# Reordering splits and additions around two seven-product blocks of a transformer layer

## The chip, the cores and the metric

The kernel runs on one core of a Trainium2 chip. The metric is the device time of one execution in microseconds (us); before the change the median of three runs is 786.5 us. TensorE (PE) multiplies matrices into PSUM; VectorE (DVE), ScalarE (ACT) and GpSimd (POOL) do elementwise work; SyncE (SP) issues most of the transfers.

## The reference

One layer on 512 tokens of width 1024, all in float32. The input is normed and multiplied by one wide matrix, and the result is cut into the parts of two branches: a gated linear attention with four heads (gla) and a latent attention with eight heads (mla). The branches are gated, summed and projected, and a squared-ReLU network follows. The change touches the first part:

```python
n = rmsnorm(h, g_mix[l])
proj = n @ w_in[l]
(gq, gk, gv, gr, z_gf, z_gb, cq, ckv, kr, z_ma, z_mb) = jnp.split(proj, SPLIT_IDX, axis=-1)
# gla: per head, forward and backward in the tokens
la_f = jax.nn.log_sigmoid((z_gf @ w_gate_f + b_gate_f).astype(jnp.float32)) / GLA_GATE_NORM
b = jnp.cumsum(log_a, axis=3)
q_dec = q * jnp.exp(b)
k_dec = k * jnp.exp(-b)
```

## The kernel before

**Split products.** A float32 operand is written as high + low, both in the format that TensorE takes (fp32r). `split` (L92) makes the high part on ACT (L93) and the low part, source minus high, on DVE (L94). A product of two split operands is three matmuls: `mm3`, L88 to L90. So each weight needs an ACT and a DVE instruction before TensorE can use it. A split weight lies in the buffers `wh` and `wl`, four of each, shared by all products of this stretch; a weight as loaded lies in `wf`, three of them. A buffer is given to the next tile when its last reader is done.

**Seven products for eight.** The products for gr (gates of gla) and gv (its values), 512 tokens by 1024 columns each, are done with seven block products in place of eight (class `Seven`). `SEVEN` gives their order: 1, 2, 5, 6, 3, 7, 4; so "the sixth product" is number 7. A weight has four blocks, and each block two halves, so `prepare(m)` makes up to two subtractions of blocks on DVE (`less`, L601) and then two splits (tiles such as gr70h and gr71l: block gr, product 7, half 0 or 1, high or low). `product(m)` runs 24 matmuls of 512 columns onto two accumulators and then takes the sums: products 1, 5, 6 are copied out by ACT (L643); behind 2, 3, 7 DVE adds the accumulator to a copy (L650), and behind 2, 3, 7, 4 the finished rows go to a `sink`. For gr that is a tanh on ACT (L659) and a multiplication on DVE (L660); for gv a scaled split (L97, L98). Products 1, 6, 7, 4 share the accumulators `xs`; product 4 must wait until DVE has read them behind product 7.

**Fillers.** Between the block products stand small projections, called fillers: zb4, the z chunk (wz, result zk; the inputs of the gates and the rotary key), gq1, gk1, zb5. Each has a load, a split of 128x1024 (wz: 128x512) and 24 matmuls (zk: 16).

**The order.** The loop over `steps` runs gr's seven products and gv's first three. In each step the operands two steps ahead are prepared, then the product of this step is run; in a step with a filler, first the filler's load and split are written, then the product, then the preparation, then the filler's matmuls. The sums of the input (xy, xz) are split in steps 1 and 2. The last four products of gv are written out by hand and mixed with the decays of head 0: `gates_begin` (two matmuls, Abs, Exp, Ln on ACT), `gates_end` (for both directions four scans L453 and a subtraction L457 on DVE, two exponentials L461 and L462 and a small one on ACT, small copies on POOL), and `gla_qk`, which multiplies q and k by the decays (L482 on DVE, L490 on POOL). The first matmuls of the scores are bd (L521).

What sets the order: `in_program_order` (called with ACT and DVE as `SPLITTERS` from `fixed` on, with TensorE from `ordered` on) makes each of these engines run its instructions in the order in which they are written, up to the end of the loop over the heads. POOL is held in order up to the gates. SP is ordered by the planner; the fillers' loads are only held behind the loads of gr's blocks.

Of the kernel before, what the change touches and what calls it, by code (L numbers as in the profile page):

```python
# [56 lines left out]
def tile_block(ctx: ExitStack, tc: tile.TileContext, t, out: bass.AP):  # L57
# [13 lines left out]
    def u4(name, dt=F32R, shape=(P, 2, S)):  # L71
        return tl(list(shape), dt, "u4", 26, name)
# [4 lines left out]
    def ps(tag, name):  # L77
        serial[0] += 1
        return pp.tile([P, S], F32, tag=tag, bufs=4, name=f"{name}_{serial[0]}")
# [343 lines left out]
            nc.sync.dma_start(kr[a + 32 : a + 48, :], kr[a : a + HALF, :])  # L423


    def gates_begin(h):

        l = u4("l", F32)
        ms = []
        for i, d in enumerate(("f", "b")):  # L430
            bcol = (V_BF if d == "f" else V_BB) + h
            bias = gvec[:, bcol : bcol + 1]
            acc = ps("mm", f"gate{d}")
            nc.tensor.matmul(acc, gates[d][:, h * P : (h + 1) * P], z4, start=True, stop=True)
            nc.scalar.activation(l[:, i], acc, AF.Abs, bias=bias)
            m = u2(f"m{d}")
            nc.vector.tensor_scalar(m, acc, bias, 0.0, op0=ALU.add, op1=ALU.min)
            ms.append(m)
        nc.scalar.activation(l, l, AF.Exp, scale=-1.0)
        nc.scalar.activation(l, l, AF.Ln, bias=1.0)  # L440
        return l, ms

    def gates_end(begun):
        l, ms = begun
        return {d: decays(d, l[:, i], ms[i]) for i, d in enumerate(("f", "b"))}

    def decays(d, l, m):
        sign = 1.0 if d == "f" else -1.0
        rr = tl([P, NT, P + 1], F32, "rr", 2, f"rr{d}")
        nc.gpsimd.memset(rr[:, :, 0:1], 0.0)  # L450
        for j in range(NT):
            c = slice(j * P, (j + 1) * P)
            nc.vector.tensor_tensor_scan(rr[:, j, 1:], m[:, c], l[:, c], 0.0, ALU.add, ALU.subtract)  # L453
        dif = u2(f"dif{d}", F32, (P, NT, P))
        off = 1 if d == "f" else 0
        mid = rr[:, :, 64:65]
        nc.vector.tensor_tensor(  # L457
            dif, rr[:, :, off : off + P], mid.to_broadcast([P, NT, P]), op=ALU.subtract
        )
        ee = u4(f"ee{d}", F32, (P, 2, NT, P))  # L460
        nc.scalar.activation(ee[:, 0], dif, AF.Exp, scale=sign * INV_NORM)  # L461
        nc.scalar.activation(ee[:, 1], dif, AF.Exp, scale=-sign * INV_NORM)  # L462
        v3 = tl([P, 3, NT], F32, "v3", 4, f"v3{d}")
        nc.gpsimd.tensor_copy(v3[:, 0, :], rr[:, :, 64])  # L464
        nc.gpsimd.tensor_tensor(v3[:, 1, :], rr[:, :, P], rr[:, :, 64], op=ALU.subtract)
        nc.gpsimd.tensor_copy(v3[:, 2, :], rr[:, :, P])
        e3 = tl([P, 3, NT], F32, "e3", 4, f"e3{d}")
        nc.scalar.activation(e3, v3, AF.Exp, scale=INV_NORM)
        return ee, e3

    def project_qk(h, x):
        col, name = ((C_GQ, "gq"), (C_GK, "gk"))[x]
        qk[h, x] = qk_normed(h, x, proj_T(col + h * P, f"{name}{h}"))

    def gla_qk(h, parts):
        near = {}
# [107 lines left out]
    class Seven:  # L584
# [17 lines left out]
                    self.blocks[dst][g], self.blocks[x][g], self.blocks[y][g], op=ALU.subtract  # L602
                )

        def prepare(self, m):

            x = {1: 0, 2: 2, 5: 0, 6: 0, 3: 3, 7: 1, 4: 2}[m]
            if m == 5:
                self.less(0, 1, 0)
            elif m == 6:  # L610
                self.less(0, 3, 0)
            elif m == 3:
                self.less(2, 2, 0)
            elif m == 7:
                self.less(1, 3, 1)
            self.right[m] = []
            for g in range(2):
                wh, wl = halves(2, S, f"{self.name}{m}{g}")
                split(wh, wl, self.blocks[x][g])
                self.right[m].append((wh, wl))  # L620

        def product(self, m):
            if m == 1:
                self.xs = [ps("at", f"{self.name}x{rb}") for rb in range(2)]
                self.c11, self.c12, self.c22 = ([u2(f"{self.name}{c}") for _ in range(2)] for c in "abc")
            elif m == 2:
                self.ws = [ps("mm", f"{self.name}w{rb}") for rb in range(2)]
            elif m == 5:
                self.zs = [ps("at", f"{self.name}z{rb}") for rb in range(2)]
            accs = {2: "ws", 5: "zs", 3: "zs"}.get(m, "xs")  # L630
            accs = getattr(self, accs)
            begin = m in (1, 2, 5)
            right = self.right.pop(m)
            for p in range(KD // 2):
                lh, ll = x_left[p][m]
                wh, wl = right[p // 2]
                for rb in range(2):
                    tok = slice(rb * P, (rb + 1) * P)
                    mm3(accs[rb], lh[:, tok], ll[:, tok], wh[:, p % 2, :], wl[:, p % 2, :],
                        begin and p == 0, p == KD // 2 - 1, not begin)  # L640
            if m in (1, 5, 6):
                for acc, c in zip(accs, {1: self.c11, 5: self.c22, 6: self.c12}[m]):
                    nc.scalar.activation(c, acc, AF.Copy)  # L643
            elif m == 4:
                for rb, acc in enumerate(accs):
                    self.sink(2 + rb, 0, acc, u2(f"{self.name}d"))
            else:
                cs = {2: self.c11, 3: self.c12, 7: self.c22}[m]
                for acc, c in zip(accs, cs):
                    nc.vector.tensor_tensor(c, acc, c, op=ALU.add)  # L650
                for rb, c in enumerate(cs):
                    self.sink(rb + (2 if m == 7 else 0), int(m != 2), c, c)

    g1, v = {}, {}
# [298 lines left out]
    def finish_zb(f, begun):  # L953
        g2.append(gated(proj_run(begun, xT), f"b{f}")[1])
# [10 lines left out]
    finish_zb(2, zb_early[0])  # L965
    sevens[0].prepare(2)
    finish_zb(3, zb_early[1])
    for n, (a, m) in enumerate(steps[:-4]):
        ahead = steps[n + 2]
        if a == 0:  # L970
            for x in {3: (0,), 7: (2, 1), 4: (3,)}.get(m, ()):
                sevens[1].load(x)
        if (a, m) in fillers:
            first_part, rest = fillers[a, m]
            at = traced()
            w = first_part()
            goes_behind((at, traced()), loading, (mybir.EngineType.SP,))
            if n == 1:
                split_sums(x_y, 5, 6)
            sevens[a].product(m)  # L980
            sevens[ahead[0]].prepare(ahead[1])
            rest(w)
            continue
        if n == 2:
            split_sums(x_z, 7, 3)
        sevens[ahead[0]].prepare(ahead[1])
        if (a, m) == (0, 5):
            load_gates()
            pos_i = u2("pos_i", I32)
            nc.gpsimd.dma_start(pos_i, t["positions"][0].partition_broadcast(P))  # L990
        if (a, m) == (0, 4):
            split_gates()
        sevens[a].product(m)
    in_program_order(summed, (mybir.EngineType.Pool,))

    gated_now = gates_begin(0)
    sevens[1].prepare(7)
    sevens[1].product(6)  # L1000
    parts = gates_end(gated_now)
    sevens[1].prepare(4)
    sevens[1].product(3)
    w_k = begin_qk(1, 1)
    sevens[1].product(7)
    w_b = begin(C_ZB + 5 * P, "zb5")
    near, nxt, far = gla_qk(0, parts)
    finish_qk(1, 1, w_k)
    sevens[1].product(4)
    w_a = begin_za(0)  # L1010
    finish_zb(5, w_b)
    ckv_, cq_ = Latent(C_CKV, 2, V_KV, "ckv"), Latent(C_CQ, 3, V_Q, "cq")
    for h in range(GH - 1):
        sc = gla_scores(near, nxt, far)
        gated_now = gates_begin(h + 1)
        w_b = begin_za(2 * h + 1)
        acc = proj_run(w_a, xT)
        if h < 2:
            w_a, lows = begin_late(C_GQ + (h + 2) * P, f"gq{h + 2}")
        else:  # L1020
            ckv_.begun[0], lows = begin_late(C_CKV, "ckv0")
        l, ms = gated_now
        parts = {"f": decays("f", l[:, 0], ms[0])}
        lows()
        parts["b"] = decays("b", l[:, 1], ms[1])
        za_gate(2 * h, acc)
        os = gla_out(h, sc)
        near, nxt, far = gla_qk(h + 1, parts)
        rs = gla_squares(h, os)
        za_gate(2 * h + 1, proj_run(w_b, xT))  # L1030
        if h < 2:
            w_b = begin_qk(h + 2, 1)
            gla_gated(h, os, rs)
            finish_qk(h + 2, 0, w_a)
            w_a = begin_za(2 * h + 2)
            finish_qk(h + 2, 1, w_b)
        else:
            ckv_.begin(1)
            gla_gated(h, os, rs)
            ckv_.run(0)  # L1040
            cq_.begin(0)
            ckv_.run(1)
        gla_turn(h)
# [413 lines left out]
```

## Time and profile before

| | us |
|---|---|
| median of 3 runs (lowest, highest) | 786.5 (786.31, 787.09) |
| the profiled execution: its own time | 789.31 |
| its span, first to last instruction | 787.6 |
| PE busy | 766.8 (97%) |
| DVE busy | 569.7 (72%) |
| ACT busy | 442.1 (56%) |
| POOL busy | 113.2 (14%) |
| mean granted clock of TensorE | 0.988 |

The profile is of one execution. A timeline line reads: start, length, engine, line of the code, operation, output<-inputs, sizes, count, and in brackets the idle time of the engine before it with what ended that. A tile's name is shown without its number, so gk stands for the projection gk1. Lengths of neighbours overlap a little: matmuls of 512 columns start every 0.227 us at full clock though each is shown 0.39 long. The granted clock is 1.00 at full speed and 0.50 when TensorE is held to half.

### The profile page before, as it was taken

What the parts mean: (1) busy time and instruction counts of PE and PEld (TensorE: products, weight loads), DVE (VectorE), ACT (ScalarE), POOL (GpSimd) and SP (SyncE); (2) the same over time, 40 slices, a digit from 0 to 9 for tenths busy, and PEclk for the clock granted to TensorE, in tenths of its full rate; (3) what the DMA queues carried; (4) which work ended last, traced back from release to release, by engine and by line L of the source; (5) the groups of instructions that cost most, each with busy time, mean ns of one, the idle gap of its engine ahead of it and who ended that gap; (6) DMA issues with size and microseconds to landing.
All of it is one profiled execution on the core that took longest, in us unless ns stands there. A gap on an engine that the chain in (4) does not pass through costs nothing.

```text
span 787.6 us, 10144 instructions
## 1 busy us (share of the span) xinstructions
PE 766.8 (97%) x3768; PEld 645.9 (82%) x3768; DVE 569.7 (72%) x850; ACT 442.1 (56%) x749; POOL 113.2 (14%) x190
## 2 busy tenths in 40 slices
PE   9998899799999999999999999999999999999996
PEld 7886678598888888888888898888888888888885
DVE  7787687747656867699983578875787477857695
ACT  7465458354647546698863376444653456436644
POOL 0710001206245204221120000000000000000014
PEclk9999899899999999999999999999999999999999
DMA  9723300113222623322124642055105511450002
GB/s 311 238 85 130 87 27 0 55 29 84 76 54 55 144 40 87 78 95 55 40 79 136 230 122 76 29 187 157 31 27 189 159 31 50 161 172 18 27 1 107
DMA packets 93185, 73.94 MB, mean 94 GB/s; under 512 B 15088, under 2 KB 74480, under 8 KB 93136
## 3 DMA queue, kind: packets, MB, share of 16 engines
q1 hardware_dynamic: 92048, 70.14, 30.2%
q10 hardware_dynamic: 864, 2.38, 0.8%
q0 software_dynamic: 224, 0.79, 0.3%
q8 instruction: 29, 0.48, 0.3%
q14 instruction: 20, 0.16, 0.1%
HBM read 69.62 MB, written 2.10 MB: 91 GB/s over the span
## 4 chain that ended last, share of the span: by engine, by line
PE 88%; DVE 6%; ACT 5%; issue 1%; POOL 0%; POOLq 0%; ACTq 0%; DVEq 0%
PE f L89 7%; PE f L88 7%; PE f L90 7%; PE gx L88 4%; PE gx L89 4%; PE gx L90 4%; PE first L325 3%; PE za L88 2%; PE wo L89 2%; PE za L89 2%; PE za L90 2%; PE wo L88 2%; PE gz L88 2%; PE gz L89 2%; PE wo L90 2%; PE gz L90 2%
## 5 line engine op out<-in xcount | busy, mean ns | idle before, releaser
L1396 POOL DMA_DIRECT2D gfin<-in_g_final x1 | 0.7, 653 | 282.6 <-PE f L90 282.6
L1221 DVE TENSOR_TENSOR w<-w,w 128x1024 f32<-128x1024 f32 x32 | 38.7, 1221 | 0.4
L893 DVE TENSOR_REDUCE top<-s 128x1 f32<-128x512 f32 x32 | 21.8, 680 | 5.2 <-PE s L90 5.1
L896 ACT ACTIVATE e<-s,top 128x512 f32<-128x512 f32 x32 | 21.8, 685 | 5.9 <-DVE top L893 3.2
L464 POOL COPY v3f<-rrf 128x4 f32<-128x4 f32 x4 | 2.8, 709 | 150.5 <-DVE rrf L453 150.5
L1168 DVE TENSOR_TENSOR h<-gx,h 128x512 f32<-128x512 f32 x32 | 21.6, 685 | 1.9 <-PE gx L90 1.8
L94 DVE TENSOR_TENSOR pT<-tp,pT 128x512 fp32r<-128x512 f32 x32 | 21.6, 679 | 0.8 <-ACT pT L93 0.7
L93 ACT ACTIVATE pT<-tp 128x512 fp32r<-128x512 f32 x32 | 19.0, 594 | 4.0 <-PE tp L910 3.8
L910 PE MATMUL tp<-ident,e 128*128 128x128 f32 x128 | 19.2, 272 | 0.2 <-DVE pT L94 0.2
L928 POOL TENSOR_TENSOR tb<-tb,za 128x512 f32<-128x512 f32 x8 | 11.2, 1401 | 55.0 <-DVE tb L927 40.6
L88 PE MATMUL av<-pT,v 128*128 128x256 f32 x64 | 19.1, 298 | 0.0
L89 PE MATMUL av<-pT,v 128*128 128x256 f32 x64 | 18.5, 289 | 0.0
L1274 ACT ACTIVATE fa<-f 128x512 f32<-128x512 f32 x32 | 18.5, 577 | 0.0
L910 PEld LDWEIGHTS tp<-ident,e 128*128 128x128 f32 x128 | 15.5, 140 | 3.6 <-PE s L90 0.8
L90 PE MATMUL av<-pT,v 128*128 128x256 f32 x64 | 18.2, 285 | 0.0
L93 ACT ACTIVATE gbh<-y 128x512 fp32r<-128x512 f32 x16 | 10.1, 633 | 14.0 <-DVE y L1291 14.0
L94 DVE TENSOR_TENSOR sc<-sc,sc 128x512 fp32r<-128x512 f32 x16 | 10.9, 690 | 9.5 <-ACT sc L93 9.5
L93 ACT ACTIVATE sc<-sc 128x512 fp32r<-128x512 f32 x16 | 9.3, 595 | 11.5 <-DVE sc L539 11.5
L88 PE MATMUL s<-kbuf,q 96*128 96x512 f32 x32 | 14.0, 437 | 1.2 <-DVE grb L708 0.9
L93 ACT ACTIVATE b_20h<-w 128x1024 fp32r<-128x1024 f32 x7 | 7.4, 1059 | 12.1 <-PE gz L90 6.0
L93 ACT ACTIVATE b_10h<-w 128x1024 fp32r<-128x1024 f32 x7 | 7.4, 1059 | 12.1 <-PE gx L90 6.0
L93 ACT ACTIVATE b_00h<-w 128x1024 fp32r<-128x1024 f32 x7 | 7.4, 1058 | 12.1 <-PE gz L90 6.0
(1569 smaller groups left out, 2893.0 us busy)
## 6 DMA issues: line engine op xcount, KB each, us to landing
w<-in_w_ff SPq DMA_DIRECT2D x64, 256.0 KB, 3.5
grw<-in_w_in SPq DMA_DIRECT2D x8, 512.0 KB, 8.6
gvw<-in_w_in SPq DMA_DIRECT2D x8, 512.0 KB, 4.3
x<-in_xt SPq DMA_DIRECT2D x8, 256.0 KB, 5.1
vw<-in_w_first SPq DMA_DIRECT2D x8, 256.0 KB, 5.3
h<-in_x ACTq DMA_DIRECT2D x4, 512.0 KB, 5.1
out<-ms SPq DMA_DIRECT2D x7, 256.0 KB, 2.3
q<-ro SPq DMA_DIRECT2D x16, 64.0 KB, 2.3
```

Source lines behind the costliest of these rows:

```text
L88: nc.tensor.matmul(acc, lh, rh, start=start, stop=False, skip_group_check=onto)
L89: nc.tensor.matmul(acc, lh, rl, start=False, stop=False, skip_group_check=onto)
L90: nc.tensor.matmul(acc, ll, rh, start=False, stop=stop, skip_group_check=onto)
L93: nc.scalar.activation(hi, src, AF.Copy)
L94: rest.tensor_tensor(lo, src, raw(hi), op=ALU.subtract)
L325: nc.tensor.matmul(f_accs[i], a[:, i * P : (i + 1) * P], b, start=k == 0 and x == 0, stop=k == KD - 1 and x == 2)
L893: nc.vector.tensor_reduce(top, acc, axis=AX.X, op=ALU.max, negate=True)
L896: nc.scalar.activation(e, acc, AF.Exp, bias=top, accum_out=tot)
L910: nc.tensor.transpose(tp[:, k * P : (k + 1) * P], e[:, k * P : (k + 1) * P], ident)
L1168: nc.vector.tensor_tensor(hc, acc, hc, op=ALU.add)
L1221: nc.vector.tensor_tensor(wq[dst][g], wq[x][g], wq[y][g], op=op)
L1274: nc.scalar.activation(a, acc, AF.Relu)
```

## The change

1. In the loop, a filler's load and split (`fillers[...][0]`) are written one step earlier than its matmuls, ahead of that earlier step's preparation.
2. `product` is cut into `multiply` (matmuls, and copies or additions behind them) and `sinks`. In the loop, at product 7 of gr, the order becomes matmuls and additions, then the preparation of gv's product 1, then the sinks.
3. The decays become a class `Gates` with single steps (`logs`, `sums`, `exps`), `prepare` is cut into `right_sums` and `right_split`, and gv's last four products with head 0's decays are written out in these steps. The loop over the other heads uses the same class in the order it had before.

The step functions hold the same instructions as before. The loop and the written-out end, old and new:

```diff
     for n, (a, m) in enumerate(steps[:-4]):
         ahead = steps[n + 2]
...
-        if (a, m) in fillers:
-            first_part, rest = fillers[a, m]
+        if steps[n + 1] in fillers:
             at = traced()
-            w = first_part()
+            begun[steps[n + 1]] = fillers[steps[n + 1]][0]()
             goes_behind((at, traced()), loading, (mybir.EngineType.SP,))
-            if n == 1:
-                split_sums(x_y, 5, 6)
-            sevens[a].product(m)
-            sevens[ahead[0]].prepare(ahead[1])
-            rest(w)
-            continue
+        if n == 1:
+            split_sums(x_y, 5, 6)
         if n == 2:
             split_sums(x_z, 7, 3)
-        sevens[ahead[0]].prepare(ahead[1])
...
-        sevens[a].product(m)
+        if (a, m) in fillers:
+            sevens[a].product(m)
+            sevens[ahead[0]].prepare(ahead[1])
+            fillers[a, m][1](begun.pop((a, m)))
+        elif m == 7:
+            sevens[a].multiply(m)
+            sevens[ahead[0]].prepare(ahead[1])
+            sevens[a].sinks(m)
+        else:
+            sevens[ahead[0]].prepare(ahead[1])
+            sevens[a].product(m)
...
-    gated_now = gates_begin(0)
-    sevens[1].prepare(7)
-    sevens[1].product(6)
-    parts = gates_end(gated_now)
-    sevens[1].prepare(4)
-    sevens[1].product(3)
+    gv = sevens[1]
+    gate = Gates(0)
+    gv.right_sums(7)
+    gv.right_split(7, 0)
+    gate.logs()
+    gv.multiply(6)
+    gate.sums("f")
+    gv.right_split(7, 1)
+    gate.exps("f")
+    gate.sums("b")
+    gv.right_sums(4)
+    gv.right_split(4, 0)
+    gate.exps("b")
+    gv.multiply(3)
     w_k = begin_qk(1, 1)
-    sevens[1].product(7)
+    gv.multiply(7)
+    near, nxt, far = gla_qk(0, gate.parts)
+    gv.right_split(4, 1)
+    gv.sinks(3)
+    gv.sinks(7)
     w_b = begin(C_ZB + 5 * P, "zb5")
-    near, nxt, far = gla_qk(0, parts)
     finish_qk(1, 1, w_k)
-    sevens[1].product(4)
+    gv.product(4)
```

More of the change, by code (lines that the diff above doesn't have):

```diff
@@ L423, in z_chunk_run @@
             nc.sync.dma_start(kr[a + 32 : a + 48, :], kr[a : a + HALF, :])
[L426 to L469, printed above, removed]
@@ L471, in project_qk, with __init__, logs, sums @@
-    def project_qk(h, x):
-        col, name = ((C_GQ, "gq"), (C_GK, "gk"))[x]
-        qk[h, x] = qk_normed(h, x, proj_T(col + h * P, f"{name}{h}"))
+    class Gates:
+        def __init__(self, h):
+            self.l = u4("l", F32)
+            self.ms = []
+            for i, d in enumerate(("f", "b")):
+                bcol = (V_BF if d == "f" else V_BB) + h
+                bias = gvec[:, bcol : bcol + 1]
+                acc = ps("mm", f"gate{d}")
+                nc.tensor.matmul(acc, gates[d][:, h * P : (h + 1) * P], z4, start=True, stop=True)
+                nc.scalar.activation(self.l[:, i], acc, AF.Abs, bias=bias)
+                m = u2(f"m{d}")
+                nc.vector.tensor_scalar(m, acc, bias, 0.0, op0=ALU.add, op1=ALU.min)
+                self.ms.append(m)
+            nc.scalar.activation(self.l, self.l, AF.Exp, scale=-1.0)
+            self.parts, self.rr, self.dif = {}, {}, {}
+        def logs(self):
+            nc.scalar.activation(self.l, self.l, AF.Ln, bias=1.0)
+        def sums(self, d):
+            i = 0 if d == "f" else 1
+            rr = tl([P, NT, P + 1], F32, "rr", 2, f"rr{d}")
+            nc.gpsimd.memset(rr[:, :, 0:1], 0.0)
+            for j in range(NT):
+                c = slice(j * P, (j + 1) * P)
+                nc.vector.tensor_tensor_scan(
+                    rr[:, j, 1:], self.ms[i][:, c], self.l[:, i, c], 0.0, ALU.add, ALU.subtract
+                )
+            dif = u2(f"dif{d}", F32, (P, NT, P))
+            off = 1 if d == "f" else 0
+            nc.vector.tensor_tensor(
+                dif, rr[:, :, off : off + P], rr[:, :, 64:65].to_broadcast([P, NT, P]), op=ALU.subtract
+            )
+            self.rr[d], self.dif[d] = rr, dif
+        def exps(self, d):
+            sign = 1.0 if d == "f" else -1.0
+            rr, dif = self.rr[d], self.dif[d]
+            ee = u4(f"ee{d}", F32, (P, 2, NT, P))
+            nc.scalar.activation(ee[:, 0], dif, AF.Exp, scale=sign * INV_NORM)
+            nc.scalar.activation(ee[:, 1], dif, AF.Exp, scale=-sign * INV_NORM)
+            v3 = tl([P, 3, NT], F32, "v3", 4, f"v3{d}")
+            nc.gpsimd.tensor_copy(v3[:, 0, :], rr[:, :, 64])
+            nc.gpsimd.tensor_tensor(v3[:, 1, :], rr[:, :, P], rr[:, :, 64], op=ALU.subtract)
+            nc.gpsimd.tensor_copy(v3[:, 2, :], rr[:, :, P])
+            e3 = tl([P, 3, NT], F32, "e3", 4, f"e3{d}")
+            nc.scalar.activation(e3, v3, AF.Exp, scale=INV_NORM)
+            self.parts[d] = ee, e3
@@ L603, in less, with right_sums @@
                 )
-        def prepare(self, m):
-            x = {1: 0, 2: 2, 5: 0, 6: 0, 3: 3, 7: 1, 4: 2}[m]
+        def right_sums(self, m):
             if m == 5:
@@ L616, in prepare, with right_split, multiply @@
             self.right[m] = []
+        def right_split(self, m, g):
+            x = {1: 0, 2: 2, 5: 0, 6: 0, 3: 3, 7: 1, 4: 2}[m]
+            wh, wl = halves(2, S, f"{self.name}{m}{g}")
+            split(wh, wl, self.blocks[x][g])
+            self.right[m].append((wh, wl))
+        def prepare(self, m):
+            self.right_sums(m)
             for g in range(2):
-                wh, wl = halves(2, S, f"{self.name}{m}{g}")
-                split(wh, wl, self.blocks[x][g])
-                self.right[m].append((wh, wl))
+                self.right_split(m, g)
         def product(self, m):
+            self.multiply(m)
+            self.sinks(m)
+        def multiply(self, m):
             if m == 1:
@@ L643, in product, with sinks @@
                     nc.scalar.activation(c, acc, AF.Copy)
-            elif m == 4:
-                for rb, acc in enumerate(accs):
-                    self.sink(2 + rb, 0, acc, u2(f"{self.name}d"))
[L647 to L651, printed above, removed]
+            elif m in (2, 3, 7):
+                for acc, c in zip(accs, {2: self.c11, 3: self.c12, 7: self.c22}[m]):
+                    nc.vector.tensor_tensor(c, acc, c, op=ALU.add)
+        def sinks(self, m):
+            if m == 4:
+                for rb, acc in enumerate(self.xs):
+                    self.sink(2 + rb, 0, acc, u2(f"{self.name}d"))
+            elif m in (2, 3, 7):
+                for rb, c in enumerate({2: self.c11, 3: self.c12, 7: self.c22}[m]):
                     self.sink(rb + (2 if m == 7 else 0), int(m != 2), c, c)
@@ L967, in tile_block @@
     finish_zb(3, zb_early[1])
+    begun = {}
     for n, (a, m) in enumerate(steps[:-4]):
@@ L1014, in tile_block @@
         sc = gla_scores(near, nxt, far)
-        gated_now = gates_begin(h + 1)
+        gate = Gates(h + 1)
+        gate.logs()
         w_b = begin_za(2 * h + 1)
@@ L1021, in tile_block @@
             ckv_.begun[0], lows = begin_late(C_CKV, "ckv0")
-        l, ms = gated_now
-        parts = {"f": decays("f", l[:, 0], ms[0])}
+        gate.sums("f")
+        gate.exps("f")
         lows()
-        parts["b"] = decays("b", l[:, 1], ms[1])
+        gate.sums("b")
+        gate.exps("b")
         za_gate(2 * h, acc)
         os = gla_out(h, sc)
-        near, nxt, far = gla_qk(h + 1, parts)
+        near, nxt, far = gla_qk(h + 1, gate.parts)
         rs = gla_squares(h, os)
```

## The prediction

> **What bounds the kernel now.** I read first where TensorE stands still: its table of waits (us in total, times, longest), for 29 to 165 us, the stretch of the two seven-product blocks, and then for 161 to 330 us.
>
> ```profile
> PE gk L88 <- ACT gk1h L93: 4.9, 1, 4.9
> PE grx L88 <- DVE grc L650: 3.1, 1, 3.1
> PE zk L411 <- DVE wzh L94: 2.8, 1, 2.8
> PE gq L90 <- DVE gq1l L94: 0.4, 1, 0.4
> ```
> ```profile
> PE s L88 <- DVE grb L708: 0.9, 1, 0.9
> ```
>
> Four waits here, all on work of ACT or DVE, and one small one behind. Next the timeline of TensorE at their edges (start, length).
>
> ```profile
> 67.36 0.39 PE L90 MATMUL grx<-gr61h,xs 128*128 128x512 f32 x1
> 70.50 5.54 PE L411 MATMUL zk<-xT,wzh 128*128 128x512 f32 x16 [2.76 <-DVE wzh L94]
> 75.88 0.39 PE L88 MATMUL grz<-gr30h,xs 128*128 128x512 f32 x1
> 81.32 0.39 PE L88 MATMUL grx<-gr70h,xs 128*128 128x512 f32 x1
> ...
> 86.53 0.39 PE L90 MATMUL grx<-gr71h,xs 128*128 128x512 f32 x1
> 90.07 0.77 PE L88 MATMUL grx<-gr40h,xT 128*128 128x512 f32 x1 [3.15 <-DVE grc L650]
> ...
> 98.31 0.39 PE L88 MATMUL gvx<-gv10h,xT 128*128 128x512 f32 x1
> ...
> 109.19 0.39 PE L88 MATMUL gq<-xT,gq1h 128*128 128x512 f32 x1
> 115.36 0.39 PE L88 MATMUL gvz<-gv50h,xs 128*128 128x512 f32 x1
> ...
> 137.35 0.39 PE L90 MATMUL gvx<-gv71h,xs 128*128 128x512 f32 x1
> 142.61 0.80 PE L88 MATMUL gk<-xT,gk1h 128*128 128x512 f32 x1 [4.88 <-ACT gk1h L93]
> 150.47 0.39 PE L88 MATMUL gvx<-gv40h,xT 128*128 128x512 f32 x1
> ...
> 161.35 1.05 PE L521 MATMUL bd<-qkb 128*128 128x128 f32 x8
> ```
>
> An undisturbed product of 24 matmuls takes 81.32 - 75.88 = 5.44 us, 0.227 each. Now the pieces beside a wait: the 16 matmuls of zk take 75.88 - 70.50 = 5.38 where 16 x 0.227 = 3.63 would do (1.75 lost); product 4 of gr takes 98.31 - 90.07 = 8.24 (2.80 lost); gq 115.36 - 109.19 = 6.17 (0.73 lost, its wait included); gk 150.47 - 142.61 = 7.86 (2.42 lost). The stretches of 3.41 us show why (length; PE, PEld, DVE, ACT, POOL busy; granted clock; DMA).
>
> ```profile
> 68.59:72.00 3.41, 1.50 (x6) 1.24 (x7) 3.41 (x5) 0.42 (x2) 0.00 (x0) 0.99 0.71 264
> 72.00:75.41 3.41, 3.41 (x9) 2.67 (x8) 1.95 (x2) 0.74 (x1) 0.00 (x0) 0.51 0.72 211
> ...
> 85.65:89.06 3.41, 1.27 (x6) 0.73 (x4) 3.15 (x4) 2.30 (x3) 0.00 (x0) 0.99 1.07 372
> 89.06:92.48 3.42, 2.41 (x6) 1.96 (x7) 2.77 (x5) 1.34 (x2) 0.00 (x0) 0.50 0.20 46
> 92.48:95.89 3.41, 3.41 (x10) 2.65 (x9) 0.00 (x0) 0.27 (x1) 0.00 (x0) 0.51 0.00 0
> ```
>
> A stretch in which TensorE idles over half is followed by one or two at half clock. So a wait costs itself and a slow restart: 2.91 + 1.75 at zk, 3.31 + 2.80 at product 4, 0.73 at gq, 5.03 + 2.42 at gk: 18.95 us in all.
>
> **The change, part by part.** No matmul, split or addition is added or taken away, and the order of TensorE stays. What moves is the order on ACT and DVE, which the kernel fixes to the program's. From the first bd matmul (161.35) on the order is unchanged and TensorE hardly waits, so I count a gain made here as kept to the end. On SP the loads of gk1, zb5 and za0 follow the release of a staging buffer by an earlier filler's split, so they come earlier, none later. POOL gets the same small copies and multiplications in the same order; it leads TensorE at bd by several us and keeps that.
>
> Parts one and two meet at product 4 of gr; these DVE and ACT rows carry them.
>
> ```profile
> 51.03 2.49 DVE L94 TENSOR_TENSOR xs<-xy,xs 128x512 fp32r<-128x512 f32 x4
> ...
> 77.22 1.22 DVE L94 TENSOR_TENSOR gr71l<-grw,gr71h 128x1024 fp32r<-128x1024 f32 x1 [3.23 <-ACT gr71h L93]
> ...
> 85.36 1.31 DVE L660 SCALAR_TENSOR_TENSOR grb<-tr,grb 128x512 f32<-128x512 f32 x2 [0.19 <-ACT tr L659]
> 86.93 1.23 DVE L94 TENSOR_TENSOR gv10l<-gvw,gv10h 128x1024 fp32r<-128x1024 f32 x1 [0.26 <-ACT gv10h L93]
> 89.24 1.28 DVE L650 TENSOR_TENSOR grc<-grx,grc 128x512 f32<-128x512 f32 x2
> ```
> ```profile
> 44.10 0.63 ACT L368 ACTIVATE tb<-zb 128x512 f32<-128x512 f32 x1 [2.38 <-DVE zb L366]
> ...
> 62.16 2.18 ACT L93 ACTIVATE xs<-xz 128x512 fp32r<-128x512 f32 x4
> ...
> 76.13 1.06 ACT L93 ACTIVATE gr71h<-grw 128x1024 fp32r<-128x1024 f32 x1 [3.39 <-PE zk L411]
> ```
>
> *Filler splits.* The split of wz stands in front of the four splits of xz (62.16 on ACT) instead of behind those of gr3. With the delay worked out next, ACT begins it near 63 and DVE has it near 64.5, so zk starts where product 6 ends, 67.36 + 0.23 = 67.59. The wait and its slow restart go; unhindered, zk ends at 71.22, product 3 at 76.66, product 7 at 82.10. DVE, busy nearly throughout, becomes the clock of this stretch. In front: the zb4 split waits for its ACT half, which follows the tanh of 44.10 and ends near 45.7; with the splits of gr5 behind it, and the copies on ACT, the xs splits start about 0.9 us later than 51.03 (an estimate from these durations). Behind: the 3.23 us that DVE waited for gr71h go, because ACT waited there for zk to release its weight buffer (76.13, zk's end) and zk now ends at 71.2. Balance: DVE is 2.3 us earlier from gr71l on.
>
> *Additions ahead of splits.* The scaling of product 3 (L660) ends at 85.36 + 1.25 = 86.6 before, 84.3 after. The two gv1 splits (86.93 to 89.24, and 0.26 of wait) leave their place, so the addition starts at 84.3 instead of 89.24. Product 4 follows its start by 90.07 - 89.24 = 0.83: at 85.1, not 90.07. That is 5.0 us gained; but TensorE has stood since 82.10, 3.0 us. The zk wait has come back here, with DVE late instead. The moved splits are not needed before product 4 ends, and the sinks of 7 feed nothing on TensorE soon.
>
> For the restart I take one half-clock stretch, 1.7 us, the price at zk after 2.91; the bounds are 0 and the 2.80 after 3.31. Gain in product 4: 2.80 - 1.7 = 1.1.
>
> The Trainium skill ("TensorE: Matmul & The Clock Gate", What's actually happening) has the clock halved only after an idle window of about 3.4 us; taken by its letter, 3.0 us would cost nothing more and the sum would be 1.7 better. The trace speaks against the letter: 2.91 us were enough at zk.
>
> *gq.* Its split moves a step ahead, in front of the splits of gv5, more than one product earlier, against a wait of 0.4. The 0.73 us go. The loads of the fillers come early anyway: wz is issued at 24.97 and 26.90, and the split needs it near 63.
>
> ```profile
> 24.97 1.89 SPq L400 DMA_DIRECT2D wzf<-in_w_in  x1
> 26.90 3.44 SPq L401 DMA_DIRECT2D wzf<-in_w_in  x1
> ```
>
> *End of the value product.* The rows that carry it:
>
> ```profile
> 121.00 1.06 ACT L93 ACTIVATE gv31h<-gvw 128x1024 fp32r<-128x1024 f32 x1 [1.66 <-PE gvz L90]
> ...
> 124.22 1.06 ACT L439 ACTIVATE l<-l 128x1024 f32<-128x1024 f32 x1
> 125.30 1.28 ACT L440 ACT_TABLE_LOAD   x1
> ...
> 141.52 1.04 ACT L93 ACTIVATE gk1h<-gk1f 128x1024 fp32r<-128x1024 f32 x1
> ```
> ```profile
> 130.91 1.37 DVE L453 TENSOR_TENSOR_SCAN rrf<-mf,l 128x128 f32<-128x128 f32 x4
> ```
>
> gk1's ACT half stood behind everything: decays, both splits of gv4, and the scaling of product 3 (L97), each waiting for DVE. Afterwards only one gv4 split and the exponentials stand ahead. Counted from the second gv3 split (121.00 = 0), with the durations quoted (a split half 1.04 and 1.22, a pair of additions 1.28, four scans 1.37, a 512-wide activation 0.63, a subtraction about as much): exp ends at 4.3; the subtraction for gv7 is done early enough for its first split at 5.2 to 6.2; the table load ends at 7.4, ln at 8.5; four scans and the difference at 10.5; DVE's second gv7 split at 11.7; scans and difference of b at 13.7; on ACT the f exponentials, one gv4 split to 14.0, the b exponentials to 15.2, gk1h to 16.2. DVE: gv40l, the additions of product 3, then gk1l to 17.6. TensorE ends product 7 at 137.58 - 121.00 = 16.6, so gk1h is in time and gk1l, needed two matmuls later at 17.0, is 0.6 late. Under half a stretch, so no slow restart. Bounds: 0, and 2.6 if four of the hand-overs between ACT and DVE on this way cost 0.5 more each. The 7.45 us at gk fall to 0.6: 6.85 gained. Next late would be the second gv4 split, behind the four multiplications by decays: it ends 2 us before its use. The sinks of 3 and 7 now end later, but the value rows are read only after 161 us.
>
> **Sum.** 5.0 + 1.1 + 0.7 + 6.85 = 13.7 us, against the profiled execution's 789.3 (span 787.6): 775.6. The median of the runs is 786.5, 2.8 lower; I carry the same gain: **772.8**. If part of those 2.8 us is clock lost in this stretch that the timed runs do not lose, the gain is smaller by at most that: 775.6.
>
> **Rivals.** Two more rows: a load of the value blocks on SP, and the landing of wz.
>
> ```profile
> 71.65 1.50 SPq L595 DMA_DIRECT2D gvw<-in_w_in  x2
> ```
> ```profile
> DMA to landing us min/median/max: 6.4/7.1/7.8
> ```
>
> - *No slow restart at product 4*: everything else the same, 1.7 less, 771.1. It needs a wait that two stretches share, each idle for less than half; the boundaries quoted (85.65, and 3.41 earlier 82.24) put nearly all of 82.1 to 85.1 into one, but another execution may have them elsewhere. 0.25. The rule of the Trainium skill cited above would give this time too.
> - *gk still waits*: the chain through ln, scans and two exponentials has some ten hand-overs between ACT and DVE. With 2 us more, 2.6 of wait and a slow restart of 1.75 replace 0.6: 3.75 more, 776.6. For it: this very queue made the longest wait of before, 4.9. Against: most of what stood ahead is gone. 0.15.
> - *Slower*: the wz load is put by the planner behind the value-block loads on SP, and its split, now in front of the splits of xz and gr3, holds both queues until it lands. Loads of wz landed up to 7.8 us after issue, and the issue takes 5.3. It decides from a landing 13.7 us after the need, 77; issued after the value blocks at 71.65 it would land at 85 to 86, 22 late, and give 795. Against: it is issued at 25 now, and its buffer is free early. 0.03.
> - *The new order does not take effect*, or its gain is lost later: 786.5. Against it, ACT and DVE are held to program order, and nothing behind 161 us waits long. 0.02.
>
> **How the numbers follow.** The chances are the rivals' above. My forecast has 0.55; by the bounds at product 4 (restart 2.80) and gk (0) its own range is 772.2 to 773.9. The range takes in the first two rivals, the bound of the sum, and about 1.5 us of error of the estimates below the first rival: 769.5 to 777.0. A measurement of this kernel can tell about 0.2% (1.6 us) from no change. Faster 0.95, within 0.2% 0.02, slower 0.03.
>
> **What would show it.** Right: no wait of TensorE before zk and gq; one of 2 to 3.5 us before product 4 of gr, on the addition L650, with a half-clock stretch behind it; under 1 us before gk; the first bd matmul near 147.7 instead of 161.35. Wrong: a wait before gk over 2 us, a wait on a DMA, or a gain here that is lost after 161 us.

## The result and the profile after

| | before | after |
|---|---|---|
| median of 4 runs (us) | 786.77 (786.31 to 787.09) | 776.20 (774.47 to 777.02) |
| ratio, 95% interval | | 0.9863 (0.9845 to 0.9881) |
| profiled execution (us) | 789.31, clock 0.988 | 774.47, clock 0.998 |
| its span (us) | 787.6 | 772.8 |

The change is worth 10.6 us, by the ratio 1.4%. The forecast was 772.8 us, 3.4 us too low; 776.2 lies inside the range and also beside the rival *gk still waits* (776.6), though not for that rival's reason.

TensorE's waits in the same stretch of after (us in total, times, longest):

```profile
PE grx L88 <- DVE grc L658: 2.7, 1, 2.7
...
PE gk L90 <- DVE gk1l L94: 0.5, 1, 0.5
PE zb L90 <- DVE zb5l L94: 0.4, 1, 0.4
PE gk L88 <- ACT gk1h L93: 0.3, 1, 0.3
```

The waits before zk and gq are gone, the one before product 4 of gr is there, and gk keeps 0.8 of 4.9. (The addition that the prediction calls L650 is L658 in the new kernel.) The wait on zb5l was not foreseen. The timeline of TensorE in after at the edges of the forecast (start, length), and one row of before:

```profile
28.53 0.39 PE L88 MATMUL zb<-xT,zb2h 128*128 128x512 f32 x1
...
66.61 1.07 PE L411 MATMUL zk<-xT,wzh 128*128 128x512 f32 x4
...
84.03 0.47 PE L88 MATMUL grx<-gr40h,xT 128*128 128x512 f32 x1 [2.75 <-DVE grc L658]
...
89.58 0.39 PE L88 MATMUL gvx<-gv10h,xT 128*128 128x512 f32 x1
...
100.47 0.39 PE L88 MATMUL gq<-xT,gq1h 128*128 128x512 f32 x1
...
105.91 0.39 PE L88 MATMUL gvz<-gv50h,xs 128*128 128x512 f32 x1
...
125.40 0.39 PE L88 MATMUL gvx<-gv71h,xs 128*128 128x512 f32 x1
...
134.97 0.39 PE L88 MATMUL gvx<-gv40h,xT 128*128 128x512 f32 x1
...
140.41 0.39 PE L88 MATMUL zb<-xT,zb5h 128*128 128x512 f32 x1
...
146.59 0.60 PE L523 MATMUL bd<-qkb 128*128 128x128 f32 x4
```
```profile
29.51 0.39 PE L88 MATMUL zb<-xT,zb2h 128*128 128x512 f32 x1
```

The rows are read in pairs. The first zb2 matmul, ahead of anything that the change touches, comes 29.51 - 28.53 = 0.98 earlier in this execution: that much of the difference of the two profiles is not the change. From the first bd matmul to the end the two spans need the same time (787.6 - 161.35 = 626.25, and 772.8 - 146.59 = 626.21), so what is gained ahead of it is kept. Between the two lie 13.78 us, term by term:

| term | forecast | measured, profile to profile |
|---|---|---|
| product 4 of gr starts earlier (after the 0.98) | 5.0 | 90.07 - 84.03 - 0.98 = 5.06 |
| slow restart in product 4 | 1.1 (2.80 to 1.7) | 8.24 - (89.58 - 84.03) = 2.69 |
| gq | 0.7 | 6.17 - (105.91 - 100.47) = 0.73 |
| gk, waits included | 6.85 (7.45 to 0.6) | 6.04 (7.45 to 1.41) |
| zb5 | 0 | 5.44 - (146.59 - 140.41) = -0.74 |
| sum | 13.7 | 13.78 |

(gk in after: product 7 ends at 125.40 + 12 x 0.227 = 128.12, and gk runs to 134.97, 6.85 later, against 5.44 undisturbed.) The sum agrees to 0.1 us with the forecast, but by luck: the restart term came out 1.6 better, and gk and zb5 together 1.55 worse. And the median moved by only 10.6. That is the question for the experiments.

### The profile page after: what moved, and what is told of

Its sections match the earlier page's. It is cut to its first block, busy times and chain, and to the rows that moved or that the text cites. A ratio compares the mean times of both kernels' runs of the same rounds, so it can differ in the third digit from the quotient of the medians.

```text
span 772.8 us, 10152 instructions
## 1 busy us (share of the span) xinstructions
PE 759.4 (98%) x3768; PEld 640.6 (83%) x3768; DVE 571.3 (74%) x850; ACT 441.8 (57%) x749; POOL 117.9 (15%) x190
## 4 chain that ended last, share of the span: by engine, by line
PE 90%; DVE 5%; ACT 2%; issue 1%; POOL 1%; POOLq 0%; ACTq 0%
PE f L89 8%; PE f L88 8%; PE f L90 8%; PE gx L88 4%; PE gx L89 4%; PE gx L90 4%; PE first L325 3%; PE za L88 2%; PE wo L90 2%; PE za L89 2%; PE wo L88 2%; PE gz L88 2%; PE za L90 2%; PE wo L89 2%; PE gz L89 2%; PE gz L90 2%
```

## The experiments

Theory: each wait is set by the DVE queue of this stretch, so a part alone moves a wait as much as it removes one; the restart behind a wait is drawn anew in each execution, and the two profiles were a dear draw of before and a cheap one of after. Rivals: that the parts do what they seem to do, each its own gain; that the gain was lost behind 146 us; and for gk, hand-overs between ACT and DVE rather than slower instructions.

### Each part alone

Three kernels undo two of the three parts of the change. *only_fill* keeps the fillers' earlier splits; *only_adds* keeps the branch below; *only_end* keeps the end in single steps.

```diff
 only_fill and only_end leave out
-        elif m == 7:
-            sevens[a].multiply(m)
-            sevens[ahead[0]].prepare(ahead[1])
-            sevens[a].sinks(m)
 only_adds and only_end split at the old place
-        if steps[n + 1] in fillers:
+        if (a, m) in fillers:
 only_fill and only_adds have the old end
+    gv.prepare(7)
+    gv.product(6)
+    for d in ("f", "b"):
+        gate.sums(d)
+        gate.exps(d)
+    gv.prepare(4)
+    gv.product(3)
...
```

> Only the fillers' splits a step earlier; the additions at product 7 of gr and the end of gv as before. My theory (DVE is what paces this stretch, so the wait at zk moves to product 4): no wait before zk and gq, but about 4.7 us before product 4 of gr on the addition, with one or two half-clock stretches behind it; the gk wait of 5 us stays; 2 to 3.5 us faster than before, 783.3 to 784.8. Rival (each wait is a term of its own): zk's 2.9 and its slow restart of 1.75 and gq's 0.7 go, product 4 keeps its 3.3: 5.4 us faster, 781.4.

> Only the additions behind product 7 of gr ahead of the splits of gv's product 1; fillers and end as before. My theory: the zk wait of 2.9 and its slow restart stay and give DVE time, so the wait before product 4 falls from 3.3 to about 0.7 and its slow restart goes: 4 to 5.5 us faster, 781.3 to 782.8. Rival (the wait before product 4 is 2.7 whatever the fillers do, as in the changed kernel): 0.6 to 3 us faster, 783.8 to 786.2.

> Only the end of the value product in single steps; fillers and additions as before. My theory: waits at zk, product 4 of gr and gq as before, and the 5 us before gk and its slow restart of 2.4 fall to 0.8 to 1.4 in all; with a wait of 0.4 before zb5 on its split: 5.3 to 6.7 us faster, 780.1 to 781.5. Rival (the end's gain hangs on the earlier parts, since the chain behind gv5 is paced by DVE's backlog): under 4 us faster.

| | median (us) | ratio, 95% | less than before |
|---|---|---|---|
| before (13 runs) | 786.66 | | |
| only_fill (10 runs) | 785.00 | 0.9976 (0.9965 to 0.9986) | 1.7 |
| only_adds (4 runs) | 782.00 | 0.9941 (0.9922 to 0.9961) | 4.7 |
| only_end (4 runs) | 780.39 | 0.9917 (0.9893 to 0.9941) | 6.3 |

TensorE's waits in the three, in this order:

```profile
PE grx L88 <- DVE grc L658: 5.4, 1, 5.4
...
```
```profile
...
PE zk L411 <- DVE wzh L94: 2.8, 1, 2.8
...
PE grx L88 <- DVE grc L658: 0.5, 1, 0.5
```
```profile
PE grx L88 <- DVE grc L658: 3.1, 1, 3.1
PE zk L411 <- DVE wzh L94: 2.8, 1, 2.8
...
```

only_adds and only_end came inside their ranges; only_fill is just above its own, and far from its rival's 781.4. The filler part takes away the wait of 2.8 before zk and makes the one before product 4 longer by 2.3 (3.1 to 5.4): 0.5 of wait is all that it gains there. The additions cut the same wait by 2.6 as long as the zk wait still gives DVE time. With both, 2.7 stay. So these two parts share one DVE queue and don't add up, while the end stands by itself.

The three alone give 12.6, together 10.6. The gap is not all DVE's queue, for the new loop has a fourth difference that the list of changes leaves out. Before, the preparation of gv's product 2 stood ahead of `split_gates` (the splits of the gate weights, `gate_f` and `gate_b`); now it stands behind, in the three kernels above as well. DVE in before, then in only_end:

```profile
100.91 0.69 DVE L393 TENSOR_TENSOR gate_f<-wgf,gate_f 64x512 fp32r<-64x512 f32 x1
...
108.92 1.23 DVE L94 TENSOR_TENSOR gq1l<-gq1f,gq1h 128x1024 fp32r<-128x1024 f32 x1 [0.69 <-ACT gq1h L93]
```
```profile
90.51 0.69 DVE L393 TENSOR_TENSOR gate_f<-wgf,gate_f 64x512 fp32r<-64x512 f32 x1
...
105.21 1.23 DVE L94 TENSOR_TENSOR gq1l<-gq1f,gq1h 128x1024 fp32r<-128x1024 f32 x1 [1.04 <-ACT gq1h L93]
```

TensorE in only_end (product 4 of gr, then gq and its successor):

```profile
88.53 0.47 PE L88 MATMUL grx<-gr40h,xT 128*128 128x512 f32 x1 [3.15 <-DVE grc L658]
...
95.70 0.39 PE L88 MATMUL gvx<-gv10h,xT 128*128 128x512 f32 x1
...
106.58 0.39 PE L88 MATMUL gq<-xT,gq1h 128*128 128x512 f32 x1
...
112.02 0.39 PE L88 MATMUL gvz<-gv50h,xs 128*128 128x512 f32 x1
```

In only_end gate_f is done while TensorE still runs product 4, and gq1l starts 105.21 - 95.70 = 9.51 behind the start of gv's product 1, in before 108.92 - 98.31 = 10.61. These 1.1 us are more than the 0.4 that gq waited, and gq takes 5.44 without a wait although its own split is at its old place; in only_adds too. So the gate splits are enough to explain the 0.73 at gq; that is read from the rows, and they were not moved alone. If each of the three kernels has these 0.73, they stand in the sum of 12.6 three times, and once in 10.6: 11.1 are left to compare.

Up to product 4 of gr, only_end runs as before does, with the same waits of 2.76 and 3.15. Yet product 4 takes 95.70 - 88.53 = 7.17 here and 8.24 there, behind the same wait. The next part asks why.

### The restart is drawn

*after_again* is the changed kernel once more, unchanged.

> The changed kernel once more, for the spread. My theory (a slow restart of 1.7 us follows the 2.7 us wait before product 4 of gr in some executions and not in others, by where the 3.4 us stretches lie): times fall into two groups some 1.7 us apart, or spread over that width, the longer ones with a mean clock about 0.002 lower; median 775.5 to 776.5. Rival (the spread has nothing to do with the clock): no relation between a run's clock and its time.

Measured: 776.54 (775.73 to 776.78), ratio 0.9873 (0.9857 to 0.9890), every run with a clock of 0.995 or 0.996; the median is just above the expected 775.5 to 776.5. Product 4 in the profile of after, then in this one (stretch, length; PE, PEld, DVE, ACT, POOL busy; granted clock; DMA):

```profile
84.03:89.58 5.55, 5.55 (x24) 4.58 (x25) 5.49 (x8) 3.75 (x6) 0.00 (x0) 1.00 0.51 154
```
```profile
84.73:91.90 7.17, 7.17 (x25) 5.72 (x25) 6.44 (x8) 3.75 (x6) 0.00 (x0) 0.76 0.41 120
```
```profile
29.25 0.39 PE L88 MATMUL zb<-xT,zb2h 128*128 128x512 f32 x1
...
84.73 0.47 PE L88 MATMUL grx<-gr40h,xT 128*128 128x512 f32 x1 [2.73 <-DVE grc L658]
```

One program, one wait (2.75 and 2.73): no slow clock in the first, 7.17 - 5.44 = 1.73 lost in the second, which is the 1.7 of the forecast. The two executions differ by 776.78 - 774.47 = 2.31; product 4 makes 1.62 of it, and the start ahead of zb2 (29.25 against 28.53) 0.72. In only_adds the zk wait of before is met by the other draw:

```profile
70.35:74.11 3.76, 3.76 (x17) 3.11 (x17) 3.44 (x3) 1.06 (x1) 0.00 (x0) 1.00 0.47 142
```

3.76 at full clock behind 2.75 of wait, where before took 5.38 behind 2.76. Of the 29 runs of before that were timed beside the experiments, the eight at a clock of 0.994 took 785.2 to 786.0 us and the two at 0.988 took 788.6 and 789.0. The profiled execution of before (0.988, 789.31) is slower than all of them; that of after (0.998, 774.47) is the fastest of eight, whose others, at 0.995 and 0.996, took 775.7 to 777.0. The mean clock alone is a weak sign, for it takes in the idle end too, where every trace shows half clock (in after it is the only place, and the mean is 0.998): late_scaling, below, has 0.997 to 0.999 at one time. That the draw differs at one and the same place is shown by the two traced executions; for the other six it is read from clock and time together.

### Taking the wait at product 4 below the restart

*late_scaling* makes DVE earlier there: the scaling of gr's product 3 goes behind the additions of product 7 and the splits of gv's product 1.

```diff
             sevens[a].multiply(m)
             sevens[ahead[0]].prepare(ahead[1])
+            sevens[a].sinks(3)
             sevens[a].sinks(m)
+        elif (a, m) == (0, 3):
+            sevens[ahead[0]].prepare(ahead[1])
+            sevens[a].multiply(m)
```

> The changed kernel with the scaling of product 3 of gr (tanh and multiplication) moved behind the additions of product 7 as well. My theory (the wait before product 4 is DVE's queue): DVE reaches those additions 1.3 to 1.5 us earlier, the wait falls from 2.7 to 1.3 us, under half of a 3.4 us stretch, so no run shows a half-clock stretch any more: mean clock 0.997 or more in every run, and against the changed kernel 1.3 us faster where that had no slow restart and 3 us where it had one: 773.2 to 774. Rival (the spread of the changed kernel's runs, 774.5 to 777.0, is not a matter of the clock): 1.3 us faster at most, with the same spread.

Measured: 773.14 (772.91 to 773.23), ratio 0.9827 (0.9808 to 0.9846). TensorE and DVE at product 4:

```profile
82.75 0.47 PE L88 MATMUL grx<-gr40h,xT 128*128 128x512 f32 x1 [1.24 <-ACT gv11h L93]
...
88.27 0.39 PE L88 MATMUL gvx<-gv10h,xT 128*128 128x512 f32 x1
```
```profile
81.92 1.28 DVE L658 TENSOR_TENSOR grc<-grx,grc 128x512 f32<-128x512 f32 x2
```

The bracket names a split on ACT, but product 4 starts 0.83 behind the start of the addition at 81.92, the step that the prediction read in before: it waits for DVE. The wait is 1.24 and product 4 takes 5.52. The gain of 3.1 to 3.4 on after is 1.5 of wait and one stretch of 1.7, and the runs now lie within 0.3 us of each other: no wait over 1.24 is left in this stretch, and its trace shows no half clock before the idle end.

*zk_between* asks whether cover does the same: on top of late_scaling the zk matmuls run between products 7 and 4, where TensorE waits.

```diff
-        (0, 6): (lambda: z_chunk_begin("mm"), z_chunk_run),
+        (0, 7): (lambda: z_chunk_begin("mm"), z_chunk_run),
...
             sevens[ahead[0]].prepare(ahead[1])
+            if (a, m) in fillers:
+                fillers[a, m][1](begun.pop((a, m)))
```

> late_scaling, with the z chunk's matmuls moved from behind product 6 of gr to between products 7 and 4, as cover for the additions. My theory (DVE paces this stretch, so cover only moves the wait): the wait before product 4 goes, but products 3 and 7 now come before their splits: some 2 us of wait before product 3, product 4 starts within 0.7 us of where it did; 773 to 774, up to 776 if a slow restart follows. Rival (TensorE paces it and only lacks cover at product 4): no wait in its place, 1.4 us less: 771.7.

Measured: 774.77 (774.68 to 775.57), 1.6 slower than late_scaling. The wait before product 4 is gone, and in its place stands one before product 3:

```profile
PE gk L88 <- ACT gk1h L93: 1.7, 1, 1.7
PE grz L89 <- DVE gr30l L94: 1.5, 1, 1.5
```

Other work on TensorE doesn't shorten a queue of DVE. The loss itself sits mostly at gk, whose wait grew from 0.3 to 1.7. That is DVE's queue again: the first split of gv7, ahead of gk1's on ACT, waits 2.41 for DVE's subtraction (1.00 in late_scaling), and DVE has hardly been idle since it took up the later zk.

### The rest at gk and zb5

Of 0.6 expected at gk 1.41 came, and 0.74 at zb5. First gk: ACT in after, then POOL in after and in before.

```profile
127.36 0.21 ACT L474 ACTIVATE e3b<-v3b 128x12 f32<-128x12 f32 x1 [0.58 <-POOL v3b L472]
```
```profile
125.72 0.18 POOL L510 COPY c3f<-e3f 128x1 f32<-128x1 f32 x1
125.84 1.21 POOL L470 COPY v3b<-rrb 128x4 f32<-128x4 f32 x1
```
```profile
134.35 0.71 POOL L464 COPY v3b<-rrb 128x4 f32<-128x4 f32 x1 [0.55 <-DVE rrb L453]
...
135.29 0.18 POOL L505 COPY c3f<-e3f 128x1 f32<-128x1 f32 x1
```

Counted from the second gv3 split (111.59 in after), every step of the forecast's chain up to the exponentials of b comes within 0.4 us of its time, the last of them at 15.2 as forecast; so the hand-overs between ACT and DVE are not the cause. Then the small exponential e3b, ahead of gk1h on ACT, waits 0.58 for POOL, and gk1h ends at 16.9 where 16.2 was forecast. POOL is late for two reasons: c3f's copies now run ahead of v3b, behind it before, so that v3b starts at 125.84 though the scans that it reads end at 124.86; and v3b takes 1.21, beside a split on DVE, and not 0.71.

Then zb5: DVE and POOL in after.

```profile
134.14 1.63 DVE L94 TENSOR_TENSOR gv41l<-gvw,gv41h 128x1024 fp32r<-128x1024 f32 x1
135.69 2.12 DVE L98 SCALAR_TENSOR_TENSOR gv<-gvb,r_x,gv 128x512 fp32r<-128x512 f32 x2
...
139.78 1.63 DVE L94 TENSOR_TENSOR zb5l<-zb5f,zb5h 128x1024 fp32r<-128x1024 f32 x1
```
```profile
136.21 1.06 POOL L492 TENSOR_TENSOR qk<-qkf,e3f 128x256 f32<-128x256 f32 x1
```

*decays_later* (on top of late_scaling) puts the multiplications by decays, which start POOL's, behind those splits:

```diff
-    near, nxt, far = gla_qk(0, gate.parts)
     gv.right_split(4, 1)
     gv.sinks(3)
     gv.sinks(7)
     w_b = begin(C_ZB + 5 * P, "zb5")
+    near, nxt, far = gla_qk(0, gate.parts)
```

> late_scaling, and the multiplications of q and k by the decays (DVE, then POOL) moved behind the second gv4 split, the gv scalings and the zb5 split. My theory (DVE was late for zb5 because its splits and scalings ran beside POOL's multiplications and took 1.63 and 1.05 us in place of 1.22 and 0.70): those take 1.22 and 0.70 again, the 0.4 us wait before zb5 goes, and zb5 takes 5.44 and not 6.2: 0.7 us less, 772.4. Rival (they are slower because of what they read, not because of POOL): durations and wait stay, 773.1 or more.

Measured: 772.49 (771.99 to 773.13), 0.65 less than late_scaling. DVE and POOL:

```profile
129.50 1.21 DVE L94 TENSOR_TENSOR gv41l<-gvw,gv41h 128x1024 fp32r<-128x1024 f32 x1
130.63 1.41 DVE L98 SCALAR_TENSOR_TENSOR gv<-gvb,r_x,gv 128x512 fp32r<-128x512 f32 x2
...
133.28 1.22 DVE L94 TENSOR_TENSOR zb5l<-zb5f,zb5h 128x1024 fp32r<-128x1024 f32 x1
```
```profile
138.49 0.61 POOL L492 TENSOR_TENSOR qk<-qkb,c3b 128x256 f32<-128x256 f32 x1
```

The same instructions are back at 1.21, 1.41 and 1.22, POOL's at 0.61, the wait on zb5l is gone, and zb5 takes 5.44. They read what they read before, so it was not that: DVE and POOL slow each other while they work side by side. But the edit does two things for zb5l: it ends the slowing, which had cost DVE 3.1 us from the first multiplication to the end of zb5l (an estimate: the starts of these instructions in after against decays_later), and it takes DVE's own four multiplications, 2.4 us without the slowing, from ahead of the split. By the rows either is more than the wait of 0.4; the run doesn't part them. Together they are zb5's 0.74.

*gk_first* (on top of late_scaling) instead puts gk1's split ahead of the exponentials of b and of gv4's first split.

```diff
     gate.sums("b")
+    w_k = begin_qk(1, 1)
+    gate.exps("b")
     gv.right_sums(4)
     gv.right_split(4, 0)
-    gate.exps("b")
     gv.multiply(3)
-    w_k = begin_qk(1, 1)
```

> late_scaling, and gk1's split written behind the scans of the second direction, ahead of that direction's exponentials and of the first gv4 split. My theory (the 0.3 and 0.5 before gk are the place of that split in ACT's and DVE's order, with POOL's small copies ahead of it): both waits go, gk takes 5.44 and not 6.4, about 1.3 us less: 771.8. Rival (gk waits for its weight buffer, or for DVE's total work): the waits stay or move to gv's product 4, within 0.3 us of 773.1.

Measured: 775.79 (775.73 to 776.14), 2.65 more than late_scaling. gk has no wait any more, as the theory had it, and a wait of 0.4 came up before gv's product 4, as the rival had it; but neither foresaw the one before zb5:

```profile
PE zb L90 <- DVE zb5l L94: 2.4, 1, 2.4
...
PE gvx L89 <- DVE gv41l L94: 0.4, 1, 0.4
```

DVE in gk_first shows where it comes from:

```profile
127.42 1.23 DVE L94 TENSOR_TENSOR gv40l<-gvw,gv40h 128x1024 fp32r<-128x1024 f32 x1 [1.56 <-ACT gv40h L93]
...
139.84 1.63 DVE L94 TENSOR_TENSOR zb5l<-zb5f,zb5h 128x1024 fp32r<-128x1024 f32 x1
```

The split of gv4 now stands behind e3b on ACT, so DVE waits 1.56 for it and everything behind it on DVE is later, the slowed instructions too: zb5l starts at 139.84, in late_scaling at 138.48. Counted from each execution's first zb2 matmul, zb5l is 1.2 later and TensorE reaches zb5 0.7 earlier, so the wait of 0.5 grows to 2.4. That draws a stretch at half clock: zb5 takes 9.74 us in place of 5.44, 7.35 of them busy.

```profile
138.52:148.26 9.74, 7.35 (x25) 5.57 (x24) 6.00 (x7) 1.84 (x3) 1.87 (x2) 0.82 0.38 108
```

*two_fixes* joins late_scaling, gk_first and decays_later, to see whether DVE's queue was what turned gk_first round.

> late_scaling with gk_first and decays_later together. My theory (gk_first was undone only because POOL's multiplications slowed the splits before zb5; with those moved away the gk waits go and nothing comes in their place): no wait before gk or zb5, 0.95 + 0.75 less than late_scaling: 771.4 to 771.8. Rival (DVE's total work behind gv5 sets the pace and the wait only moves on): a wait of 0.5 to 1 us before gv's product 4, zb5 or bd; 772.3 or more.

Measured: 771.38 (770.73 to 771.86), ratio 0.9805 (0.9788 to 0.9822). The edit that cost 2.65 alone gains 1.1 once DVE has neither the slowing nor the multiplications ahead of zb5l. Only the 1.2 before product 4 stay.

### The best version

*three_fixes* is two_fixes with DVE's and ACT's small work of the z chunk taken out of the queue before product 4 too, behind the additions of product 7.

```diff
+        return acc
+
+    def z_chunk_tail(acc):
         both = u2("zkl")
...
             sevens[ahead[0]].prepare(ahead[1])
+            z_chunk_tail(z_acc)
             sevens[a].sinks(3)
```

> two_fixes, and the elementwise tail of the z chunk (an ACT copy, two DVE operations, an ACT copy, two more DVE operations) moved behind the additions of product 7 and the gv1 splits. My theory (what is left of the wait before product 4 is DVE's queue, down to the 0.85 us that one addition and its hand-over take at least): the wait falls from 1.25 to 0.7 us as listed, 0.5 us less than two_fixes: 770.9 to 771.4. Rival (the 1.25 is that least already): no change against two_fixes.

Measured: 770.23 (770.08 to 770.86), ratio 0.9793 (0.9777 to 0.9809): 16.4 us under before and 6.0 to 6.3 under the change. The gain on two_fixes is 1.15, twice what was expected. DVE and TensorE there:

```profile
80.72 1.37 DVE L661 TENSOR_TENSOR grc<-grx,grc 128x512 f32<-128x512 f32 x2 [1.19 <-PE grx L90]
```
```profile
80.97 0.39 PE L90 MATMUL grx<-gr71h,xs 128*128 128x512 f32 x1
81.56 0.47 PE L88 MATMUL grx<-gr40h,xT 128*128 128x512 f32 x1 [0.20 <-DVE grc L661]
```

DVE now waits for TensorE. I had held 0.85 from the end of product 7 to product 4 for the least; the first accumulator is finished before product 7's last matmuls, so the addition starts at 80.72, ahead of the end at 81.20, and product 4 follows that end by 0.36.

## Why the prediction was right in its parts and 3.4 us low

- *What bounds the kernel.* Right: waits with the restart behind them, in this stretch alone.
- *Filler splits.* Right: zk starts at 66.61, where 67.59 less the 0.98 of this execution puts it, without a wait.
- *Additions ahead of splits.* Right, 5.06 for 5.0; the wait of 3.0 was 2.9, counted as the forecast counts it (2.75 in the bracket). "The zk wait has come back here" is shown by only_fill and only_adds.
- *The restart at product 4*, one stretch of 1.7: right in after_again (1.73) and, by clock and time, probably in the other six runs at 0.995 and 0.996; in the profiled run of after nothing, as in the rival *No slow restart*. The rival's reason, that another execution may have its boundaries elsewhere, was right, but one drawn outcome is no property of the kernel.
- *gq.* Right in size, the cause not separated. "The 0.73 us go" because gq's split moves ahead; only_adds and only_end lose them with that split at its old place; by the rows the gate splits, which stand earlier too and which the prediction didn't count, are enough. The changed kernel has both moves.
- *gk and what comes next.* The chain through ln, scans and exponentials was right; the term was 0.81 too good (1.41 for 0.6). The step that failed at gk is "POOL gets the same small copies and multiplications in the same order": the order of POOL's copies changed, v3b was slowed, and ACT waited 0.58 for them, which the chain put at nothing. The share of each is read from the rows, not tried by itself. "Next late would be the second gv4 split" named the wrong instruction: it was zb5l, 0.74. There the forecast took durations from rows where DVE or POOL was alone, and put the multiplications moved ahead of zb5l at nothing; decays_later shows the two together.
- *From the profile to the median*: "I carry the same gain" is the step that cost most. Take the execution of after that has the forecast's restart, 776.78: it is 789.31 - 776.78 = 12.53 below the profile of before, where 13.7 were forecast; gk and zb5, less 0.26 of start, make up the 1.2. The remaining difference is the other end: the profiled before lies 789.31 - 786.77 = 2.54 above its median, and in it zk had drawn half clock and product 4 two stretches of it, where executions of other kernels drew none (zk in only_adds) and one (product 4 in only_end) behind the same waits. The text gave that as a bound, 775.6, and then did not use it as its value.
- *Slower* and *The new order does not take effect* did not come: no wait on a transfer, and the end behind 146.59 is unchanged.

## What to carry to other kernels

A profile is one execution: where waits of about one clock window are what a change removes, compare the profile with the median of its runs first, and charge the restart by how often the clocks of those runs show it. Where two edits relieve the same engine's queue, count that queue's work once and ask where the wait appears next; an edit that looks bad alone (gk_first) can gain once the queue is free. When instructions move beside another engine's, take their durations from rows in which both engines run. When a loop is rewritten, compare the order of every call in it: a move that nobody meant (the gate splits) can look like the work of another.

## What the runs showed of the hardware

- A wait of 2.7 to 2.8 us halved TensorE's clock for one stretch of 3.41 us in some executions (zk in before, product 4 in after_again) and not in others (zk in only_adds and only_end, product 4 in after); 3.15 did in both profiles that have it (before, only_end), 4.9 to 5.4 in every profile, 1.2 to 1.7 in none. The Trainium skill ("TensorE: Matmul & The Clock Gate", What's actually happening) says that the window of about 3.4 us runs freely and isn't reset when a kernel starts, which fits a draw by execution. Its table asks for an idle window of about 3.4 us before the clock falls; by the runs here 2.4 us (gk_first) were enough.
- DVE's splits of 128x1024 went from 1.22 to 1.63, its pairs of L98 from 1.41 to 2.12, POOL's multiplications from 0.61 to 1.06 when the two ran side by side (decays_later, then after). The Trainium skill ("SBUF — State Buffer", Who interferes with whom) has a DVE instruction with two SBUF inputs contend with a GpSimd instruction that reads SBUF. The trace agrees, and adds the price: about a third to a half on DVE, three quarters on POOL.
